# Loads of stored token sums moved within and between two DMA queues, and values staged through a wider ring of rows, in a hybrid convolution and attention step

## The chip, the cores and the metric

The kernel runs on one core of a Trainium2 chip. The metric is the device time of one execution, in microseconds (us). The times of before are three runs; one more execution was recorded by the hardware profiler, and all rows quoted below come from that one.

## The reference

One layer of a network is computed for two groups of tokens that share the weights: 128 prompt tokens and 512 latent tokens, 640 columns in all, with 1024 channels. Cut to what matters here:

```python
h = x * (1 + scale) + shift                      # modulation
z = h @ w_in                                     # 10 blocks of 1024 columns
hy, g_h, qkv, g_a, m = split(z)
hy = short_conv(hy)                              # 3 taps along the tokens
v_h, x1, x0 = split(hy); q, k, v = split(qkv)
y_h = (fft_conv(v_h * x1, filters) + v_h * x1 * d) * x0
y_a = attention(q, k, v)                         # window, context and prompt
p_h = (y_h * silu(g_h)) @ w_bh ; p_a = (y_a * silu(g_a)) @ w_ba
out = (sigmoid(m_h) * p_h + sigmoid(m_a) * p_a) @ w_out
y = layer_norm(alpha * x + gate * out)
```

The outputs are `y`, and the keys and values of the prompt.

## The kernel before, in words

All matrix products run on TensorE in a split form: each operand is kept as a high part and a low part, and a product is three matmuls (high by high, high by low, low by high). Tokens are the moving side in two halves of 320 columns, weights the stationary side in blocks of 128 by 128. `hH` and `hL` hold the high and low part of `h`, eight channel tiles of 128 by 640.

The work has three stages.

**Transform stage.** Projections for the convolution branch (`proj`, L183), the filter spectra and the transforms (`long_conv`, `long_conv_back`), and the values `v` (`values`, L656) are woven together; here a scheduler chooses the order of each engine's instructions. Beside it VectorE forms four sums of blocks of `h`: with `h` cut into 2 by 2 blocks (channel half by token half), `t1`, `t2`, `t3` and `t4` are sums and differences of those blocks. Each sum has four rows of 128 by 640 (320 KB): channel part 0 and 1 (the `r` in `load_sums(r, ...)`), each as a high and a low part. They are written to `tok_d` in device memory (`token_sums`, L725) and loaded back later. The name `t4_10` is the sum `t4`, part 1, high. The values of groups 1 to 3 go from PSUM through a staging tile (L688 to L690, ScalarE) to `v_d` in device memory (L691, L692).

**Attention stage.** From L1393 on the order of all engines and queues is the order in which the code is written (`manual_schedule`). A pair of weight tiles (256 output columns) is computed by `pair_tile` with seven products instead of eight, twelve matmuls each. Their moving operands, in this order, are those of `ORDER` (L1130): `("b11", "t2", "t3", "t1", "b21", "t4", "b22")`; a `b` is a block of `hH` and `hL` itself. So the second, third, fourth and sixth product of a pair read loaded sums. `operand` (L1122) gives the tile: in a product over a sum the four channel tiles `k` are taken in order, `k` 0 and 1 from the rows of part 0, `k` 2 and 3 from part 1, and for each `k` the matmuls read high, low, high. The four sums stay in SBUF for all 23 pairs; only the first pair meets them while they are being loaded. The weights of a pair are loaded plain by SyncE's queue (`ra`, `s2`, `rb`: `load_a`, `blocks`), and two blocks get a second weight block added to them by an accumulating DMA on GpSimd's queue (`summed`, L1163, L1164). `high` (ScalarE, L1185) and `low` (VectorE, L1193) make the split weights four products ahead; `sum1` (L1175) and `post` (L1210) are further VectorE work of a pair. `scratch` (L919) copies two half tiles of `hH` and of `hL` within SBUF.

**Last stage.** Branch projections, output projection and layer norm.

The loads that the change touches stand at three places: `hand_over` (L864) loads `t2` and `t3` of part 0; L1346 to L1348 load `t2` and `t3` of part 1 around the weights of the second pair (`load_b(1)`); L1398 to L1403 load `t1` and `t4` of both parts, behind `scratch()`. All of them go to SyncE's queue through `load_to` (L64). Each load takes a row from one of three pools: `yhp` (tag `yh`, nine rows, which also served x0, the products `yu` and the stored sums in the transform stage), `sp` (four rows `tr`) and `tp` (three rows `tr`); a load has to wait until the work that used this memory earlier is done. A DMA on SyncE's queue also waits for the one issued eight places before it to be complete, since eight semaphores are used in turn; GpSimd's queue has eight others.

Of the kernel before, what the change touches and what calls it, by code (L numbers as in the profile page):

```python
# [10 lines left out]
F32 = mybir.dt.float32  # L11
# [8 lines left out]
NK = 8  # L20
# [6 lines left out]
NG = LP + 1 + LS  # L27
# [19 lines left out]
def tile_hyena_natten_step(ctx: ExitStack, tc: tile.TileContext, a, o):  # L47
    nc = tc.nc
    P = 128

    def f(ap):
        return ap.bitcast(F32)
# [10 lines left out]
    def load_to(dst, src):  # L63
        ins = nc.sync.dma_start(dst, src)  # L64
        last[:] = [ins]
        if pinned[0]:
            tc.keep_in_program_order(ins)
# [38 lines left out]
    def row(pool, tag, name, dt=F32, bufs=NK + 1, n=NT):  # L106
        return pool.tile([P, NT + 4 if tag == "yh" else NT], dt, tag=tag, bufs=bufs, name=name)[:, :n]
# [548 lines left out]
    def values(m, home=None):  # L656
# [25 lines left out]
        if home is None:  # L682
            v = out[f"v{m}"] = slot(m, "v", f"v{m}")
            for c, p in ((0, parts[0]), (512, parts[1]), (1024, pe[:, :256])):
                nc.scalar.activation(v[:, c : c + p.shape[-1]], p, AF.Copy)
        else:
            for i, p in enumerate(parts):
                v = hwa.tile([P, NG + 1], F32, tag="cv", bufs=2, name=f"v{m}_{i}")  # L688
                nc.scalar.activation(v[:, :512], p, AF.Copy)  # L689
# [198 lines left out]
    ac = ctx.enter_context(ExitStack())  # L888
    edges, biases = {}, {}

    homes = []

    def load_sums(r, names):
        for name in names:
            for i in range(2):
                pool, tag, bufs = homes.pop(0) if r else (yhp, "yh", NK + 1)
                t = row(pool, tag, f"{name}_{r}{i}", F32R, bufs)
                tok[name][i].append(t)
                load_to(f(t), tok_d[4 * SUMS.index(name) + 2 * r + i])

    def attention_setup():
        nonlocal at, sp, tp
        hy.close()
        sp = ac.enter_context(tc.tile_pool(name="sp", bufs=1, reuse_waits="tile", side="right"))
        tp = left.enter_context(tc.tile_pool(name="tp", bufs=1, reuse_waits="tile"))
        homes[:] = [(sp, "tr", 4)] * 4 + [(tp, "tr", 3)] * 3 + [(yhp, "yh", NK + 1)]
# [487 lines left out]
    with tc.manual_schedule(engines=engines):  # L1394
        for _ in first_head():
            pass
        sums_of_second()
        scratch()  # L1398
        load_sums(0, SUMS[2:3])
        load_sums(1, SUMS[2:3])  # L1400
        load_a(1)
        load_sums(0, SUMS[3:])
        load_sums(1, SUMS[3:])  # L1403
        biases[0] = [bias_tile(h) for h in range(2)]
        for j in range(8):
            side, n_main, n_side = attend(j), N_PAIR * len(HEADS[j].split()), N_ATT if j < 7 else N_ATT + 3
# [323 lines left out]
```

## Time and profile before

| what | value |
|---|---|
| median of three runs | 885.01 us (885.0 to 885.81) |
| the profiled execution, its own time | 886.28 us |
| its span, first to last instruction | 884.5 us |
| mean granted TensorE clock | 0.992 |
| TensorE busy | 866.5 us, 98% |
| VectorE / ScalarE / GpSimd busy | 652.4 / 450.0 / 188.9 us |
| DMA queue of SyncE (q1): moved, share of the 16 DMA engines | 123.59 MB, 41.4% |
| DMA queue of GpSimd (q0): moved, share | 38.28 MB, 22.1% |

In rows of the timeline the columns are start, duration, engine, line, operation, output<-input, shape and count, and in brackets the idle time of the engine before it with what ended it. In rows of the table by windows they are the window, its length, then per engine the busy time with the number of instructions, the granted clock (PEclk), the mean busy share of the 16 DMA engines, and GB/s. In a list of waits they are the total in us, the number and the longest. Rows of DMA issues give the count, the size of one, and the median time in us from issue to landing. Tile numbers are left out, so that all sums read `t`.

### The profile page before, as it was taken

What the parts mean: (1) busy time and instruction counts of PE and PEld (TensorE: products, weight loads), DVE (VectorE), ACT (ScalarE), POOL (GpSimd) and SP (SyncE); (2) the same over time, 40 slices, a digit from 0 to 9 for tenths busy, and PEclk for the clock granted to TensorE, in tenths of its full rate; (3) what the DMA queues carried; (4) which work ended last, traced back from release to release, by engine and by line L of the source; (5) the groups of instructions that cost most, each with busy time, mean ns of one, the idle gap of its engine ahead of it and who ended that gap; (6) DMA issues with size and microseconds to landing.
All of it is one profiled execution on the core that took longest, in us unless ns stands there. A gap on an engine that the chain in (4) does not pass through costs nothing.

```text
span 884.5 us, 17176 instructions
## 1 busy us (share of the span) xinstructions
PE 866.5 (98%) x6452; PEld 836.1 (95%) x6452; DVE 652.4 (74%) x1243; ACT 450.0 (51%) x964; POOL 188.9 (21%) x216
## 2 busy tenths in 40 slices
PE   8999999999999997999999999999999999999996
PEld 6899999999999996999999999999999999999885
DVE  4778986596794855786877777777777487667666
ACT  4396465436555533666566656666666532243200
POOL 0012210110110111354353334333554200000000
PEclk9999999999999998999999999999999999999999
DMA  8978886456564778967676758675854587445521
GB/s 319 403 171 223 219 239 131 95 156 136 134 150 98 207 175 268 325 164 248 163 245 155 228 147 254 146 203 161 237 138 119 183 293 253 158 157 201 186 78 57
DMA packets 76110, 168.56 MB, mean 191 GB/s; under 512 B 11099, under 2 KB 29275, under 8 KB 76028
## 3 DMA queue, kind: packets, MB, share of 16 engines
q1 hardware_dynamic: 56780, 123.59, 41.4%
q0 software_dynamic: 13632, 38.28, 22.1%
q10 hardware_dynamic: 5616, 5.61, 1.9%
q8 instruction: 51, 0.84, 0.4%
q14 instruction: 31, 0.25, 0.1%
HBM read 142.80 MB, written 23.99 MB: 189 GB/s over the span
## 4 chain that ended last, share of the span: by engine, by line
PE 93%; DVE 3%; DMA 1%; ACT 1%; issue 0%; SPq 0%; POOL 0%; POOLq 0%; ACTq 0%
PE sp L1232 32%; PE mm L183 32%; PE out L1540 6%; PE v L669 4%; PE s L1044 2%; PE s L951 2%; PE pt L1035 2%; PE ve L680 1%; PE adaT L253 1%; DMA v_d<-v 1%; DMA t<-tok_d 1%; PE adaT L270 1%; PE yb L171 1%; PE yb L173 1%; PE yb L172 1%; PE ut L547 1%
## 5 line engine op out<-in xcount | busy, mean ns | idle before, releaser
L1232 PE MATMUL sp<-t,wb 128*128 128x320 f32 x1104 | 176.5, 313 | 5.4 <-DMA t<-tok_d 5.4
L1232 PEld LDWEIGHTS sp<-t,wb 128*128 128x128 f32 x1104 | 165.6, 189 | 7.3 <-issue 5.4
L1232 PE MATMUL sp<-hH,wb 128*128 128x320 f32 x548 | 132.9, 314 | 0.0
L1232 PEld LDWEIGHTS sp<-hH,wb 128*128 128x128 f32 x548 | 95.0, 190 | 2.6 <-issue 2.6
L1232 PE MATMUL sp<-hL,wb 128*128 128x320 f32 x274 | 85.1, 311 | 0.0
L163 POOL DMA_DIRECT2D wl<-wall x30 | 26.7, 890 | 239.2 <-ACT wl L162 174.8
L183 PE MATMUL mm<-hH,wh 128*128 128x320 f32 x288 | 69.4, 313 | 1.5 <-ACT v L689 0.8
L183 PE MATMUL mm<-hH,wl 128*128 128x320 f32 x288 | 69.5, 311 | 0.4 <-DVE wl L103 0.4
L183 PE MATMUL mm<-hL,wh 128*128 128x320 f32 x288 | 69.7, 311 | 0.0
L1193 DVE TENSOR_TENSOR wb<-s,wb 128x512 fp32r<-128x512 f32 x69 | 49.2, 714 | 22.7 <-ACT wb L1185 22.4
L1185 ACT ACTIVATE wb<-s 128x512 fp32r<-128x512 f32 x69 | 43.5, 632 | 35.7 <-PE sp L1232 20.2
L1006 POOL TENSOR_SCALAR edge<-edge,sm 128x320 f32<-128x320 f32 x32 | 42.1, 1437 | 68.0 <-DVE sm L1004 68.0
L1006 POOL TENSOR_SCALAR p<-p,sm 128x384 f32<-128x384 f32 x32 | 49.2, 1599 | 29.3 <-DVE sm L1004 14.5
L164 ACT ACTIVATE wh<-raw 128x1024 fp32r<-128x1024 f32 x30 | 31.9, 1063 | 42.0 <-PE mm L183 32.5
L1232 PEld LDWEIGHTS sp<-hL,wb 128*128 128x128 f32 x274 | 52.1, 190 | 0.0
L183 PEld LDWEIGHTS mm<-hH,wh 128*128 128x128 f32 x288 | 48.5, 188 | 3.0 <-ACT v L689 1.0
L183 PEld LDWEIGHTS mm<-hH,wl 128*128 128x128 f32 x288 | 48.9, 188 | 1.3 <-DVE wl L103 0.9
L183 PEld LDWEIGHTS mm<-hL,wh 128*128 128x128 f32 x288 | 49.0, 188 | 0.7 <-DVE hL L330 0.5
L1540 PE MATMUL out<-woh,yhs 128*128 128x512 f32 (+1 forms) x176 | 45.7, 373 | 0.0
L1220 DVE TENSOR_TENSOR spare_hHp<-sp,yu 128x320 f32<-128x320 f32 x69 | 33.4, 483 | 16.6 <-PE sp L1232 11.1
L183 PE MATMUL mm<-yhs,wh 128*128 128x320 f32 x224 | 42.6, 309 | 0.0
L1185 ACT ACTIVATE wb<-ra 128x512 fp32r<-128x512 f32 x46 | 29.1, 633 | 25.8 <-PE sp L1232 10.7
(412 smaller groups left out, 2251.1 us busy)
## 6 DMA issues: line engine op xcount, KB each, us to landing
raw<-wall SPq DMA_DIRECT2D x50, 512.0 KB, 3.8
wl<-wall POOLq DMA_DIRECT2D x30, 512.0 KB, 7.0
ra<-wall SPq DMA_DIRECT2D x23, 512.0 KB, 4.3
rb<-wall SPq DMA_DIRECT2D x44, 256.0 KB, 5.3
ada<-wada SPq DMA_DIRECT2D x16, 512.0 KB, 8.0
tm<-bias SPq DMA_DIRECT2D x16, 512.0 KB, 7.8
s<-wall SPq DMA_DIRECT2D x23, 256.0 KB, 4.9
s<-wall POOLq DMA_DIRECT2D x23, 256.0 KB, 4.4
```

What stands on the lines that cost most here:

```text
L163: nc.gpsimd.dma_start(wl, a["wall"][i], accum_op=ALU.add)
L164: nc.scalar.activation(wh, raw[:], AF.Copy)
L183: nc.tensor.matmul(ps[hf][:, :HALF], wt[k], x[:, hf * HALF : (hf + 1) * HALF], start=(i == 0 and k == 0), stop=(i == lead[2] and k == NK - ...
L669: nc.tensor.matmul(ps[t // 2][:, t % 2 * 256 : t % 2 * 256 + 256], x[:, k, P * t : P * t + P], wk, start=first and t % 2 == 0, stop=last, ...
L951: nc.tensor.matmul(dst[h], x[rows(h), qs], y[rows(h), ks], start=i == 0, stop=i == 2, skip_group_check=True)
L1006: nc.gpsimd.tensor_scalar_mul(pv, pv, sm[:, 2, c : c + 1])
L1035: nc.tensor.transpose(pt[:, i * P : i * P + P], ps[h][:, c : c + P], ident)
L1185: nc.scalar.activation(made[g][:, 0], block(g), AF.Copy)
L1193: nc.vector.tensor_tensor(made[g][:, 1], block(g), f(made[g][:, 0]), op=ALU.subtract)
L1220: nc.vector.tensor_tensor(c, dst, c if j == 3 else ps["u"], op=ALU.add)
L1232: nc.tensor.matmul(dst, wk, x(xi, k), start=j < 4 and k == 0 and i == 0, stop=k == 3 and i == 2, skip_group_check=True,)
L1540: ins = nc.tensor.matmul(dst, m[k][:, c0 : c0 + P], w[:, c : c + n], start=(first and k == 0), stop=(last and k == 5), skip_group_check=True,)
```

## The change

Three things are changed.

The loads of the sums are moved. `t2` and `t3` of part 1 are now loaded one after the other, and `t1` of both parts comes directly behind them, ahead of the plain weight loads of the second pair and ahead of `scratch`. `t4` of both parts is taken off SyncE's queue: GpSimd issues these four loads, behind its two accumulating loads for the second pair.

The homes are changed with it: `t1` takes the three rows of `tp` and one row of `yhp`, and `t4` takes four rows of `yhp`. Before, `tp` held `t1` of part 1 and one row of `t4`.

The values of groups 1 to 3 are staged in rows of the nine-row ring `yhp` instead of the two tiles `cv` of the pool `hwa`.

```diff
             for i, p in enumerate(parts):
-                v = hwa.tile([P, NG + 1], F32, tag="cv", bufs=2, name=f"v{m}_{i}")
+                v = row(yhp, "yh", f"v{m}_{i}", n=NG + 1)
...
-    def load_sums(r, names):
+    def load_sums(r, names, by=None):
...
-                pool, tag, bufs = homes.pop(0) if r else (yhp, "yh", NK + 1)
+                if r and name in SUMS[:2]:
+                    pool, tag, bufs = sp, "tr", 4
+                elif name == "t1" and (r, i) != (1, 1):
+                    pool, tag, bufs = tp, "tr", 3
+                else:
+                    pool, tag, bufs = yhp, "yh", NK + 1
...
+                if by is None:
+                    load_to(f(t), src)
+                else:
+                    by.dma_start(f(t), src)
...
-    load_sums(1, SUMS[:1])
+    load_sums(1, SUMS[:2])
+    for r in range(2):
+        load_sums(r, SUMS[2:3])
     sums_of_second = load_b(1)
-    load_sums(1, SUMS[1:2])
...
         sums_of_second()
+        for r in range(2):
+            load_sums(r, SUMS[3:], nc.gpsimd)
         scratch()
-        load_sums(0, SUMS[2:3])
-        load_sums(1, SUMS[2:3])
         load_a(1)
-        load_sums(0, SUMS[3:])
-        load_sums(1, SUMS[3:])
```

SyncE's queue before, at the passage from the transform to the attention stage, from the last two rows of `t3` on (`new_kT` is a store of keys, `hH` and `hL` are the copies of `scratch`, `ra1` is a weight tile of the second pair):

```order
L64 DMA t3_10_4037<-tok_d_81 128x640
L64 DMA t3_11_4039<-tok_d_81 128x640
L843 DMA new_kT<-kp0_4171 128x128
L64 DMA hH_85<-hHp_86 128x320 x2
L64 DMA hL_87<-hLp_88 128x320 x2
L64 DMA t1_00_4192<-tok_d_81 128x640
L64 DMA t1_01_4194<-tok_d_81 128x640
L64 DMA t1_10_4196<-tok_d_81 128x640
L64 DMA t1_11_4198<-tok_d_81 128x640
L64 DMA ra1_4200<-wall 128x1024
L64 DMA t4_00_4202<-tok_d_81 128x640
L64 DMA t4_01_4204<-tok_d_81 128x640
```

Two more rows of `t4` and the bias tiles `tm0` and `tm1` follow there. The same queue and place now (`s2_1` and `rb1` are the plain weight loads of the second pair, which before stood between `t2` and `t3`):

```order
L64 DMA t3_11_4034<-tok_d_81 128x640
L64 DMA t1_00_4036<-tok_d_81 128x640
L64 DMA t1_01_4038<-tok_d_81 128x640
L64 DMA t1_10_4040<-tok_d_81 128x640
L64 DMA t1_11_4042<-tok_d_81 128x640
L64 DMA s2_1_4045<-wall 128x512
L64 DMA rb1_4044<-wall 128x512 x2
L843 DMA new_kT<-kp0_4179 128x128
L64 DMA hH_85<-hHp_86 128x320 x2
L64 DMA hL_87<-hLp_88 128x320 x2
L64 DMA ra1_4208<-wall 128x1024
L64 DMA tm0_4210<-bias 128x1024
```

`t1` has moved ahead of the store of keys and of `scratch`, the weight loads have moved behind `t1`, and no row of `t4` is left on this queue. GpSimd's queue before, at the same passage (`yu` are products of the convolution branch, `edge` are cleared borders, L1163 and L1164 the accumulating loads of the second and then the third pair):

```order
L524 DMA yu_d_79<-yu6_3837 128x640
L524 DMA yu_d_79<-yu7_3842 128x640
L912 MEMSET edge00_3887 128x64
L912 MEMSET edge01_3889 128x64
L912 MEMSET edge30_3891 128x64
L912 MEMSET edge31_3893 128x64
L1163 DMA s2_1_4033<-wall 128x512
L1164 DMA rb1_4032<-wall 128x512
L1163 DMA s2_2_4292<-wall 128x512
L1164 DMA rb2_4291<-wall 128x512
```

And now, from the last cleared border on (line numbers are higher by six here):

```order
L918 MEMSET edge31_3893 128x64
L1169 DMA s2_1_4045<-wall 128x512
L1170 DMA rb1_4044<-wall 128x512
L906 DMA t4_00_4194<-tok_d_81 128x640
L906 DMA t4_01_4196<-tok_d_81 128x640
L906 DMA t4_10_4198<-tok_d_81 128x640
L906 DMA t4_11_4200<-tok_d_81 128x640
L1169 DMA s2_2_4292<-wall 128x512
L1170 DMA rb2_4291<-wall 128x512
```

The four rows of `t4` stand between the accumulating loads of the second and of the third pair. In the transform stage the scheduler sets many instructions of all engines in another order than before; from the first pair on the order of TensorE is the same as before, and that of VectorE and ScalarE but for a few rows at its start.

More of the change, by code (lines that the diff above doesn't have):

```diff
@@ L889, in tile_hyena_natten_step @@
     edges, biases = {}, {}
-    homes = []
-    def load_sums(r, names):
+    def load_sums(r, names, by=None):
         for name in names:
             for i in range(2):
-                pool, tag, bufs = homes.pop(0) if r else (yhp, "yh", NK + 1)
+                if r and name in SUMS[:2]:
[4 more added lines that the diff above has]
+                    pool, tag, bufs = yhp, "yh", NK + 1
                 t = row(pool, tag, f"{name}_{r}{i}", F32R, bufs)
                 tok[name][i].append(t)
-                load_to(f(t), tok_d[4 * SUMS.index(name) + 2 * r + i])
+                src = tok_d[4 * SUMS.index(name) + 2 * r + i]
+                if by is None:
+                    load_to(f(t), src)
+                else:
+                    by.dma_start(f(t), src)
     def attention_setup():
@@ L905, in attention_setup @@
         tp = left.enter_context(tc.tile_pool(name="tp", bufs=1, reuse_waits="tile"))
-        homes[:] = [(sp, "tr", 4)] * 4 + [(tp, "tr", 3)] * 3 + [(yhp, "yh", NK + 1)]
         at = ac.enter_context(tc.tile_pool(name="at", bufs=1, reuse_waits="tile", side="right"))
```

## The prediction

> **What bounds the kernel now.** The page comes first: which engine fills the span.
>
> ```profile
> PE 866.5 (98%) x6452; PEld 836.1 (95%) x6452; DVE 652.4 (74%) x1243; ACT 450.0 (51%) x964; POOL 188.9 (21%) x216
> ```
>
> TensorE is busy for 98% of 884.5 us, so only its idle time, and time at a lower clock, can be won. The list of TensorE's waits says for what it was idle.
>
> ```profile
> PE sp L1232 <- DMA t<-tok_d: 5.4, 4, 4.6
> ...
> PE mm L183 <- ACT v L689: 0.8, 1, 0.8
> PE fb L171 <- ACT sh L102: 0.5, 1, 0.5
> ```
>
> The first is what the change aims at, four waits for loaded sums; the second of the rows is a wait for a staging tile of the values, which the change touches too. TensorE's timeline shows the place of the four: the seven products of the first pair.
>
> ```profile
> 339.92 0.31 PE L1232 MATMUL sp<-hH,wb 128*128 128x320 f32 x1
> ...
> 341.68 3.71 PE L1232 MATMUL sp<-t,wb 128*128 128x320 f32 x24
> 350.03 0.61 PE L1232 MATMUL sp<-t,wb 128*128 128x320 f32 x1 [4.65 <-DMA t<-tok_d]
> ...
> 353.75 1.70 PE L1232 MATMUL sp<-t,wb 128*128 128x320 f32 x5 [0.18 <-DMA t<-tok_d]
> ...
> 358.19 1.92 PE L1232 MATMUL sp<-t,wb 128*128 128x320 f32 x12
> ...
> 361.80 0.33 PE L951 MATMUL s<-k,q 64*128 64x128 f32 x2
> ```
>
> The first product (no sum) takes 339.92 to 341.68, 12 matmuls, 0.147 us each. `t2` and `t3` follow without a gap and end at 345.39. Then `t1` is missing: four waits in one product, one per row. `t4` (358.19) waits for nothing, as the wait before it gave it time. The four products from 345.39 to the first attention matmul (361.80) take 16.4 us; at 0.147 us a matmul they would take 48 x 0.147 = 7.0. So 9.4 us is the most that this place can give. The windows of 2 us tell why it is more than the 5.4 of idle time, and what the DMA engines did meanwhile.
>
> ```profile
> 334.00:336.00 2.00, 2.00 (x15) 2.00 (x15) 1.30 (x3) 1.16 (x2) 0.00 (x0) 1.00 0.88 311
> ...
> 340.00:342.00 2.00, 2.00 (x16) 2.00 (x15) 1.65 (x8) 2.00 (x9) 1.89 (x7) 1.00 0.55 200
> ...
> 344.00:346.00 2.00, 1.39 (x10) 1.12 (x8) 2.00 (x5) 0.63 (x1) 0.00 (x0) 1.00 1.06 195
> ...
> 348.00:350.00 2.00, 0.00 (x0) 0.00 (x0) 0.05 (x1) 0.00 (x0) 0.00 (x0) 0.50 1.00 366
> ...
> 354.00:356.00 2.00, 2.00 (x8) 2.00 (x9) 0.26 (x1) 0.92 (x2) 0.00 (x0) 0.50 1.02 405
> 356.00:358.00 2.00, 2.00 (x9) 2.00 (x9) 1.90 (x5) 0.80 (x3) 0.00 (x0) 0.54 1.05 421
> ```
>
> After the gap the granted clock is 0.50 until about 357.85 (0.54 in the window to 358), some 4.1 us behind the last gap (353.75); a matmul then takes 0.268 us (8 or 9 in a 2 us window). And the DMA engines are as good as full from 344 on: shares of 1.00 to 1.06 in these rows. Only 340 to 342 has room, 0.55. So the place is limited by all that the 16 engines have to move, not by one queue's turn. This is what I weigh most.
>
> **The change, part by part.** First the fourth product's sums, `t1`. SyncE's timeline (start, duration of the issues) and the row for tile `t` give where they stood.
>
> ```profile
> 332.88 0.80 SPq L64 DMA_DIRECT2D t<-tok_d  x2
> ...
> 334.20 0.90 SPq L64 DMA_DIRECT2D rb<-wall  x2
> ...
> 341.16 1.17 SPq L64 DMA_DIRECT2D hH<-hHp  x2
> 342.37 1.93 SPq L64 DMA_DIRECT2D hL<-hLp  x2
> 344.43 4.05 SPq L64 DMA_DIRECT2D t<-tok_d  x4
> 348.52 0.43 SPq L64 DMA_DIRECT2D ra<-wall  x1
> 349.05 2.59 SPq L64 DMA_DIRECT2D t<-tok_d  x4
> 351.73 0.62 SPq L64 DMA_DIRECT2D tm<-bias  x1
> ```
>
> For all twelve rows of the three pools the trace has their first and last issue and the time to landing:
>
> ```profile
> L64 SPq DMA_DIRECT2D t<-tok_d x12: 325/468/1527, 332.9 to 351.0; - x12
> DMA to landing us min/median/max: 3.0/5.3/7.4
> ```
>
> `t1` was issued from 344.43 on, behind the copies of `scratch`. Now eight rows of 320 KB (2.62 MB) go out in a row from about 332 on; at the 0.311 MB/us of window 334 to 336 they need 8.4 us, the last lands at about 341. TensorE wants `t1` at 345.4. Even with 3 us lost to the stores of `yu` beside them they are in time: all four waits of `t1` go. The new order also puts seven more matmuls of the transform stage behind the last use of the memory that the loads take, so they can start 7 x 0.147 = 1.0 us earlier against the first product.
>
> What is late next is the sixth product, `t4`. TensorE comes to it at 345.4 + 24 x 0.147 = 348.9, after `t1` and a product without sums. Before, its last row was issued at 351.0 and, with the longest time to landing (7.4), was in at 358.4, close to where its product starts. Now GpSimd issues `t4` behind its accumulating loads, which need the plain loads of `s2` and `rb` that now stand behind `t1`.
>
> ```profile
> 340.01 1.23 POOL L524 DMA_DIRECT2D yu_d<-yu  x2 [19.15 <-DVE yu L475]
> 341.58 0.94 POOL L1163 DMA_DIRECT2D s<-wall  x1
> 342.15 1.28 POOL L1164 DMA_DIRECT2D rb<-wall  x1
> ...
> yu_d<-yu POOLq DMA_DIRECT2D x2, 320.0 KB, 3.4
> ...
> s<-wall POOLq DMA_DIRECT2D x1, 256.0 KB, 5.7
> rb<-wall POOLq DMA_DIRECT2D x1, 256.0 KB, 6.5
> ```
>
> Three plain loads of 256 KB (0.79 MB, 2.5 us at the same rate) land at about 343.5, so the accumulating loads go out at about 343.5 to 344.5 (before 341.58 and 342.15), and four issues of some 0.6 us put `t4` out from 344.5 to 347 or a little later (the homes of its last two rows also wait for the last stores of `yu`, issued at 340.01, 3.4 us to landing: 343.4 to 344.6, no later than that). The issue is 3 to 4 us earlier than before (349.05 to 351.0). But the landing is not: in front of the last row of `t4` the DMA engines still have to move the same bytes, the copies of `scratch`, the accumulating loads, `t1`, `ra`, `t4`. From 342 to 358.4 they were full, so I count their work: end before 358.4, less 0.9 for the idle part of 340 to 342 (2 us x 0.45), less 1.0 for the earlier start, plus what now overtakes. That is the two bias tiles `tm`, formerly behind `t4` on one queue, now beside it on the other. They are 512 KB each, 1.05 MB, 2.4 us at the 0.421 to 0.405 MB/us of 354 to 358. How much of them gets ahead depends on how the engines share two queues. The DMA table for 344.4 to 348.5, when both were loaded, reads:
>
> ```profile
> q0 software_dynamic: 278, 0.50, 69.6%
> q1 hardware_dynamic: 352, 0.48, 36.2%
> ```
>
> Equal bytes (0.50 and 0.48 MB) from both. GpSimd's queue holds 4 x 0.33 + 0.5 = 1.8 MB; SyncE's 0.64 (copies, 4 x 160 KB) + 0.52 (`ra`) = 1.2 MB before `tm`. By equal bytes about half of `tm` is moved when `t4` is in: +1.2, bounds 0 and 2.4. The last row of `t4` lands at 358.4 - 0.9 - 1.0 + 1.2 = 357.7 (356.5 to 358.9). The Trainium skill's page "DMA: Bandwidth & Descriptors", section "Issuing engines are not separate DMA queues", speaks against a gain from the other queue: loads started by different engines run on the same 16 engines and interleave, and only the issuing time is saved. The trace agrees, 69.6% and 36.2% filled the engines together; by that page alone the landing would be unchanged but for the order.
>
> TensorE then idles from 348.9 on for the rows of part 0, and runs at half clock behind the gap, as before for `t1`. Behind the last row stand half of a product and the seventh: 5 matmuls and 12, of which 15 fit into the 4.1 us at 0.268 and 2 go at 0.147: 4.4 us. End 357.7 + 4.4 = 362.1, against 361.80: **+0.3** (-0.9 to +1.5). The stall moves from the fourth product to the sixth and is not shortened.
>
> Second, the values.
>
> ```profile
> 199.53 0.60 ACT L689 ACTIVATE v<-v 128x512 f32<-128x512 f32 x1 [5.56 <-DMA v_d<-v]
> 200.18 0.41 PE L183 MATMUL mm<-hH,wh 128*128 128x320 f32 x1 [0.75 <-ACT v L689]
> ```
>
> ScalarE waited 5.56 us for the store of an earlier staging tile; TensorE behind it 0.75. With nine rows this goes: **-0.75**. In exchange rows of x0, `yu` and values wait for each other's stores; ScalarE is busy 51% and the other short wait of that list, on `sh`, is 0.5, so I take 0. The new order of the transform stage can gain little more than such a wait and lose two or three of them: 0, bounds -1.0 and +1.5 as an estimate.
>
> Sum: +0.3 - 0.75 = -0.45, and 886.28 becomes 885.8. The profiled execution lies 1.27 over the median; the prediction stands to the median: 885.01 - 0.45 = **884.6 us**, the likeliest case's own range 883.0 to 886.6 (landing bounds and a part of the re-ordering).
>
> **The rivals.** *A, `t4` comes early* (0.28). GpSimd's queue is served better than by equal bytes, or `tm` stays behind: the four rows land at most 6.5 us (the `rb` row) behind their issue at 347, so by 353.5. Then the second pair's `ra` is next: VectorE's `post` for the fifth product, which the seventh needs, stands behind the weights made from `ra`.
>
> ```profile
> ra<-wall SPq DMA_DIRECT2D x1, 512.0 KB, 6.5
> 355.08 0.63 ACT L1185 ACTIVATE wb<-ra 128x512 fp32r<-128x512 f32 x1 [10.31 <-DMA ra<-wall]
> ...
> 356.35 0.48 DVE L1220 TENSOR_TENSOR spare_hHp<-sp,spare_hHp 128x320 f32<-128x320 f32 x1
> ```
>
> With `ra` as late as before, the seventh product starts at 356.8 and ends at 358.6 to 360.0; with `ra` issued 4 us earlier, landing order decides and 357.9 (353.5 + 4.4) is the end. So -1.8 to -3.9; I take -2.0, as `ra` now shares the engines with `t4`. With the values: 885.01 - 2.75 = 882.3. For it speaks that before, `s` took only 5.7 and `rb` 6.5 us on that queue in the full stretch; against it, that 1.3 MB cannot go in 6 us through half of 0.4 MB/us.
>
> *B, `t4` comes later than before* (0.18). All of `tm` is moved ahead of the last row, and the earlier start is lost to the plain loads that hold up the accumulating ones: 358.4 + 2.4 = 360.8, end 365.2, +3.4, with the values +2.65: 887.7. It decides from a landing of 359.7 on. For it: `t4` is last on its queue and starts only when `s2` and `rb` are in. Against it: 0.9 us of idle engine time that the early loads must fill. The same skill page, section "Queues, rings and completion order", has each engine go round the queues packet by packet; no run here shows the turns by themselves, but by that rule the queue with larger packets gets more, and the table above has 1.8 KB a packet on GpSimd's queue and 1.4 on SyncE's, which is for A rather than B.
>
> *C, the transform stage loses* (0.09). A store of values, which took ScalarE 5.56 us of waiting, now holds a row that x0 or `yu` needs, and TensorE waits there: from 1.5 us on the kernel is slower. With a loss of 2.6, the +0.3 of the stall and no gain on the values it gives 887.9, near B's time. *The change does not do what it says* would be `t1`'s rows of `tp` becoming free too late; their earlier users stand far ahead of this place in the order, so 0.01, at 885.0.
>
> **How the numbers follow.** Forecast 0.44, A 0.28, B 0.18, C 0.09, no effect 0.01. A measurement of this kernel tells about 0.2%, 1.77 us. Faster by more than that, below 883.24: A, and 0.01 of the forecast's lower edge: 0.29. Slower, above 886.78: B and C: 0.27. Within: the rest of the forecast and no effect: 0.44. The range reaches from 881.6 (A with 357.9 and half of its sharing loss) to 888.0 (B and C, with 0.3 of re-ordering); outside remain A's best (-3.9 and -0.75: 880.4) and both losses together, 2 in 10.
>
> **What would show it.** Right: the first matmul of `t1` stands without brackets at about 345; brackets `<-DMA t<-tok_d` stand before the sixth product, from 348 on, the clock falls to 0.50 there, and attention starts within 1.2 us of 361.8 (less any shift of the first product); `t4` (now a row of GpSimd's queue) takes 8 to 12 us to landing; the wait on L689 is gone. Wrong: the sixth product starts before 353 (A), or `t4` lands behind 359.7 (B), or new waits of L183 appear between 90 and 340 (C). If `t1` still waits, the time of its loads was wrong.

## The result, and the profile after

The changed kernel takes 888.96 us (median, 888.34 to 890.08); before took 885.0 us beside it. The ratio is 1.0046, with a 95% interval of 1.0029 to 1.0064: slower, by 3.95 us. The forecast was 884.6 us and no change that can be measured, with a range up to 888.0. The profiled execution took 890.08 us (span 888.3), 3.8 more than the one of before, and all terms below are differences between these two.

TensorE's waits in the changed kernel, as a list of total, number and longest:

```profile
PE sp L1238 <- DMA t<-tok_d: 7.4, 3, 6.1
...
PE mm L183 <- ACT zs L486: 0.8, 1, 0.8
PE mm L183 <- ACT zs L485: 0.7, 1, 0.7
```

The wait for loaded sums has grown from 5.4 to 7.4 us, and the wait for a staging tile of the values (0.8) has gone, but two new ones of 0.8 and 0.7 stand in the list. TensorE's timeline of the first pair shows where the sums are waited for now:

```profile
340.72 0.31 PE L1238 MATMUL sp<-hH,wb 128*128 128x320 f32 x1
...
342.48 5.45 PE L1238 MATMUL sp<-t,wb 128*128 128x320 f32 x36
...
355.80 0.60 PE L1238 MATMUL sp<-t,wb 128*128 128x320 f32 x1 [6.11 <-DMA t<-tok_d]
357.29 2.17 PE L1238 MATMUL sp<-t,wb 128*128 128x320 f32 x6 [0.88 <-DMA t<-tok_d]
359.90 1.70 PE L1238 MATMUL sp<-t,wb 128*128 128x320 f32 x5 [0.44 <-DMA t<-tok_d]
...
364.73 0.47 PE L957 MATMUL s<-k,q 64*128 64x128 f32 x2
```

The row of 36 matmuls without a bracket is `t2`, `t3` and `t1`: the fourth product waits no more. The three rows with brackets are the sixth product. Attention starts at 364.73 instead of 361.80, 2.93 later. Of that, 0.80 was lost before the first product (340.72 against 339.92), and the stretch from the first product to attention takes 24.01 us instead of 21.88, 2.13 more. From there to the end of the execution, 890.08 - 364.73 = 525.35 against 886.28 - 361.80 = 524.48, another 0.87 is lost. 0.80 + 2.13 + 0.87 = 3.80.

The windows over the stall (window, length, busy time of the five engines, granted clock, DMA share, GB/s) answer to those of before:

```profile
352.00:354.00 2.00, 0.00 (x0) 0.00 (x0) 0.00 (x0) 0.14 (x1) 0.00 (x0) 0.50 1.04 345
...
360.00:362.00 2.00, 2.00 (x8) 2.00 (x9) 0.37 (x1) 0.32 (x1) 0.00 (x0) 0.50 0.77 285
362.00:364.00 2.00, 2.00 (x9) 2.00 (x8) 1.76 (x7) 1.36 (x6) 1.54 (x2) 0.50 0.03 9
364.00:366.00 2.00, 2.00 (x17) 1.67 (x18) 0.49 (x1) 1.09 (x2) 0.25 (x1) 0.65 1.02 165
```

The last column but one says most: the DMA engines are full up to 360 and then all but idle, 0.03 from 362 to 364. In the changed kernel the last row of `t4` lands near the end of this stretch (issued at 348.9, 11.0 us to landing: 359.9), and loads that nobody needs yet are moved ahead of it. SyncE's timeline names them:

```profile
345.78 0.83 SPq L64 DMA_DIRECT2D ra<-wall  x1
346.72 1.17 SPq L64 DMA_DIRECT2D tm<-bias  x2
...
348.68 0.76 SPq L64 DMA_DIRECT2D ra<-wall  x1
349.53 0.78 SPq L64 DMA_DIRECT2D s<-wall  x1
350.74 0.92 SPq L64 DMA_DIRECT2D rb<-wall  x2
```

GpSimd's timeline of the changed kernel shows when `t4` was issued:

```profile
344.21 0.89 POOL L1169 DMA_DIRECT2D s<-wall  x1 [1.52 <-DMA s<-wall]
346.36 0.88 POOL L1170 DMA_DIRECT2D rb<-wall  x1 [1.25 <-DMA rb<-wall]
346.92 2.51 POOL L906 DMA_DIRECT2D t<-tok_d  x4
```

Behind `ra` of the second pair (345.78) SyncE now issues not only the two bias tiles but, from 348.68 to 351.7, the weights of the third pair. In the kernel before, the same loads went out behind `t4`, by SyncE's timeline:

```profile
355.05 0.33 SPq L64 DMA_DIRECT2D ra<-wall  x1
355.86 0.33 SPq L64 DMA_DIRECT2D s<-wall  x1
356.65 1.15 SPq L64 DMA_DIRECT2D rb<-wall  x2
```

The DMA table of the changed kernel for the stretch in which `t4` is under way (347 to 360) has packets, MB and share of the engines:

```profile
q1 hardware_dynamic: 1118, 2.69, 57.2%
q0 software_dynamic: 557, 1.74, 45.8%
```

SyncE's queue (q1) moved 0.95 MB more than the queue that carried `t4`. The third pair's loads left 6.4 us earlier than before because a DMA on SyncE's queue waits for the one eight places ahead of it. Before, that one was, for the third pair's `ra`, the second pair's `ra`, which was in at 355.0 (issued at 348.52, 6.5 us to landing). With the four loads of `t4` gone it is the first copy of `scratch`; for the `s` behind it, it is the second, which was in at 349.4, and `s` left at 349.53.

### The profile page after: what moved, and what is told of

Read it like the earlier page. It is cut to its first block, busy times and chain, and to the rows that moved or that the text cites. A ratio compares the mean times of both kernels' runs of the same rounds, so it can differ in the third digit from the quotient of the medians.

```text
span 888.3 us, 17175 instructions
## 1 busy us (share of the span) xinstructions
PE 867.8 (98%) x6452; PEld 837.3 (94%) x6452; DVE 654.8 (74%) x1243; ACT 449.2 (51%) x964; POOL 190.9 (21%) x220
## 4 chain that ended last, share of the span: by engine, by line
PE 93%; DVE 3%; DMA 2%; ACT 1%; issue 0%; POOL 0%; POOLq 0%; ACTq 0%
PE sp L1238 32%; PE mm L183 31%; PE out L1545 6%; PE v L669 5%; PE s L1050 2%; PE s L957 2%; PE pt L1041 2%; PE ve L680 1%; DMA t<-tok_d 1%; PE adaT L253 1%; DMA yu_d<-yu 1%; PE adaT L270 1%; PE yb L171 1%; PE yb L173 1%; PE yb L172 1%; PE ut L547 1%
## 5 line engine op out<-in xcount | busy, mean ns | idle before, releaser
L183 PE MATMUL mm<-hH,wh 128*128 128x320 f32 x288 | 71.6, 314 | 2.3 <-ACT zs L486 0.8
L183 PE MATMUL mm<-hH,wl 128*128 128x320 f32 x288 | 70.6, 311 | 0.4 <-DVE wl L103 0.4
L183 PE MATMUL mm<-hL,wh 128*128 128x320 f32 x288 | 70.2, 311 | 0.0
L1012 POOL TENSOR_SCALAR p<-p,sm 128x384 f32<-128x384 f32 x32 | 48.3, 1554 | 29.6 <-DVE sm L1010 15.4
L183 PEld LDWEIGHTS mm<-hH,wh 128*128 128x128 f32 x288 | 49.1, 189 | 4.6 <-ACT zs L485 1.4
L183 PEld LDWEIGHTS mm<-hH,wl 128*128 128x128 f32 x288 | 49.1, 188 | 1.1 <-DVE wl L103 0.9
L183 PEld LDWEIGHTS mm<-hL,wh 128*128 128x128 f32 x288 | 49.0, 189 | 0.9 <-DVE hL L330 0.5
L183 PE MATMUL mm<-yhs,wh 128*128 128x320 f32 x224 | 42.7, 309 | 0.0
```

Of the source, the lines that this page charges most:

```text
L183: nc.tensor.matmul(ps[hf][:, :HALF], wt[k], x[:, hf * HALF : (hf + 1) * HALF], start=(i == 0 and k == 0), stop=(i == lead[2] and k == NK - ...
L1012: nc.gpsimd.tensor_scalar_mul(pv, pv, sm[:, 2, c : c + 1])
```

## The experiments

Two theories of the 2.13 us. **S (sharing)**: what SyncE's queue issues, no longer standing behind `t4`, takes the engines from it. **I (issue)**: `t4` is issued too late, behind accumulating loads that wait for `rb`. (The first expectation below also names a theory B, of the bytes ahead of `t4`; these runs do not tell it from S.) For the 0.80 us ahead of the first product: **V**, the values' new homes; **L**, the moved loads.

All runs together. The ratio is to before, measured anew beside each group of runs, with its 95% interval; runs of different groups are compared by it. The other columns are from the one profiled execution of each: when the first product starts, when the last group of matmuls of the sixth product starts after its last wait, and the time from the first product to attention. A start in brackets is one without a wait. Where eleven matmuls are left behind the last wait (355.75, 354.35 and 354.55 in the runs with `t1` early and with both held), that wait is for the second row of `t4` and the last row is in before TensorE asks for it; elsewhere it is for the last row. The profiled execution is often not the median one (its own time stands last), so that verdicts go by the ratio.

| run | median us | ratio | first product | last group of the sixth | to attention | profiled |
|---|---|---|---|---|---|---|
| before | 885.0 to 885.6 | 1 | 339.92 | (358.19) | 21.88 | 886.28 |
| changed | 888.96 | 1.0046 (1.0029 to 1.0064) | 340.72 | 359.90 | 24.01 | 890.08 |
| t1 early, t4 on SyncE behind ra | 885.20 | 0.9994 (0.9985 to 1.0003) | 340.22 | 354.35 | 19.15 | 884.14 |
| t4 on SyncE around ra | 885.91 | 1.0004 (0.9995 to 1.0013) | 341.91 | 358.43 | 21.07 | 887.74 |
| t4 ahead of the accumulating loads | 888.12 | 1.0033 (1.0020 to 1.0045) | 340.18 | 354.46 | 21.76 | 887.45 |
| bias and third pair held | 885.92 | 1.0006 (0.9997 to 1.0015) | 340.33 | 354.55 | 19.05 | 884.77 |
| third pair held | 888.52 | 1.0031 (1.0020 to 1.0041) | 341.14 | 359.75 | 22.11 | 888.52 |
| bias held | 887.62 | 1.0019 (1.0009 to 1.0028) | 341.26 | 357.60 | 21.14 | 887.58 |
| mirror | 892.33 | 1.0072 (1.0057 to 1.0087) | 340.35 | 362.34 | 26.57 | 892.10 |
| values alone | 886.27 | 1.0008 (0.9999 to 1.0017) | 341.90 | (358.92) | 20.64 | 886.95 |
| loads alone | 889.37 | 1.0038 (1.0026 to 1.0051) | 339.48 | 359.85 | 25.13 | 890.01 |
| t1 early, old values | 885.86 | 1.0002 (0.9993 to 1.0010) | 340.62 | 355.75 | 20.11 | 885.86 |
| split, held, old values | 889.25 | 1.0036 (1.0023 to 1.0050) | 339.13 | 355.93 | 21.51 | 886.41 |

**`t1` early, `t4` on SyncE's queue.** Against the changed kernel:

```diff
         sums_of_second()
-        for r in range(2):
-            load_sums(r, SUMS[3:], nc.gpsimd)
         scratch()
         load_a(1)
+        load_sums(0, SUMS[3:])
+        load_sums(1, SUMS[3:])
```

> The changed kernel, but t4 stays on SyncE's queue: behind scratch come ra of the second pair, the four rows of t4, then the bias tiles. Theory S (sharing): in the changed kernel t4 was late because SyncE's queue, freed of t4, ran ahead with the bias tiles and the third pair's weights and took 2.69 MB of the engines while GpSimd's queue moved 1.74 MB (347 to 360 us). Then here, with t4 ahead of them on one queue, its last row lands at about 356 instead of 359.8 and the kernel takes about 885.5 us, 3.5 less than the changed one. Theory I (late issue): t4 was late because it was issued at 346.9 to 349.4, behind accumulating loads that waited for rb. Here SyncE can issue it no earlier than about 346.5, so the time stays within 1 us of 888.96. Theory B (bytes): the engines' work up to t4's last row is what counts; it is less by tm and the third pair here too, so as S.

The time is 885.20 us and the gain over the changed kernel 0.0052 of 885, 4.6 us by the ratios. The last wait of the sixth product ends at 354.35. SyncE's timeline of this run:

```profile
345.82 2.30 SPq L64 DMA_DIRECT2D t<-tok_d  x4
348.22 1.32 SPq L64 DMA_DIRECT2D tm<-bias  x2
...
352.78 0.33 SPq L64 DMA_DIRECT2D ra<-wall  x1
```

And TensorE's, the sixth product and the first attention matmul:

```profile
353.61 0.39 PE L1238 MATMUL sp<-t,wb 128*128 128x320 f32 x1 [4.42 <-DMA t<-tok_d]
354.35 3.33 PE L1238 MATMUL sp<-t,wb 128*128 128x320 f32 x11 [0.36 <-DMA t<-tok_d]
...
359.37 0.33 PE L957 MATMUL s<-k,q 64*128 64x128 f32 x2
```

`t4` is issued from 345.82, 5.6 us after the first product, against 346.92 and 6.2 in the changed kernel. Its last row lands at 355.6 (issued at 347.7, 7.9 us), 15.4 us after the first product instead of 19.2. An issue 0.6 us earlier does not explain 3.8; the bias tiles are behind it now, and the third pair's weights go out at 352.78. So the whole loss of the changed kernel hangs on the queue of `t4`. That speaks for S, though `t4` also changed its queue and the way it is issued.

**Part 0 of `t4` ahead of `ra`, part 1 behind it**, on SyncE's queue:

```diff
         scratch()
+        load_sums(0, SUMS[3:])
         load_a(1)
-        load_sums(0, SUMS[3:])
-        load_sums(1, SUMS[3:])
+        load_sums(1, SUMS[3:])
```

(against the run before).

> As the run before, but part 0 of t4 stands ahead of ra of the second pair and part 1 behind it, on SyncE's queue. S: the sixth product starts at about 352 and waits a second time for part 1; ra then lands by 355 and the seventh product ends near 360; time about 884.5 us. I: issue of part 0 at about 345.5, 1.4 us earlier than in the changed kernel, so 1 to 1.5 less than it, about 887.5.

885.91 us: between the two expected times, 884.5 and 887.5, and not distinguishable from the run before. The sixth product does start a little earlier, 11.7 us after the first (353.59) instead of 13.4, but then it waits for part 1 until 358.43. In this profile, what is put ahead of `ra` is paid for by what comes behind it.

**`t4` ahead of the accumulating loads**, on GpSimd's queue; this takes away the late issue and leaves the sharing:

```diff
-        sums_of_second()
         for r in range(2):
             load_sums(r, SUMS[3:], nc.gpsimd)
+        sums_of_second()
```

> The changed kernel with one thing changed: GpSimd issues t4 ahead of its two accumulating loads of the second pair, not behind them. I: part 0 is then issued at about 342.5, 4.4 us earlier; part 1 once the yu stores are in, about 348; the sixth product starts 3 to 4 us earlier, the kernel takes about 886 us. S: SyncE's queue overtakes as before, and the accumulating loads now come behind t4, so that the second pair's sums hold up VectorE and with it the seventh product: no gain, 888 to 890 us.

888.12 us, about 1 us better than the changed kernel (0.0013 of 885), which is not clear of noise. The issue moved as I expected (342.06 and 346.18), and the sixth product started at 349.75 instead of 355.80. But the time did not follow. VectorE's timeline in this run says why:

```profile
349.15 0.49 DVE L1226 TENSOR_TENSOR spare_hHp<-sp,yu 128x320 f32<-128x320 f32 x1 [3.27 <-PE sp L1238]
356.63 0.69 DVE L1181 TENSOR_TENSOR s<-s,rb 128x512 f32<-128x512 f32 x1 [6.98 <-DMA s<-wall]
...
357.84 0.48 DVE L1226 TENSOR_TENSOR spare_hHp<-sp,spare_hHp 128x320 f32<-128x320 f32 x1
```

And TensorE's, the end of the sixth product and the start of the seventh:

```profile
354.46 1.70 PE L1238 MATMUL sp<-t,wb 128*128 128x320 f32 x5 [0.96 <-DMA t<-tok_d]
358.47 0.60 PE L1238 MATMUL sp<-hH,wb 128*128 128x320 f32 x1 [2.31 <-DVE spare_hHp L1226]
```

The accumulating loads now stand behind `t4`; `sum1` (L1181), which adds their results, is waited for until 356.63; behind it in VectorE's order stands `post`, which the seventh product needs. This is the chain of rival A, with the second pair's sums in the place of `ra`. The issue was late (I is right that far), but what waits for the accumulating loads is next, so that `t4` ahead of them won little here. What an earlier issue is worth by itself this run does not show, as it also delays the sums.

**What shares the engines with `t4`, held back.** In the changed kernel GpSimd issues the first two bias tiles, and the plain loads of the third pair, behind `t4` on its own queue:

```diff
-        load_to(tm[:], a["bias"][hd])
+        (nc.gpsimd.dma_start if hd < 2 else load_to)(tm[:], a["bias"][hd])
...
-    load_to(raws["a", p][:], a["wall"][pairs[p][0]])
+    (nc.gpsimd.dma_start if p == 2 else load_to)(raws["a", p][:], a["wall"][pairs[p][0]])
...
+        load = nc.gpsimd.dma_start if p == 2 else load_to
-        load_to(s2, w0[:, :512])
+        load(s2, w0[:, :512])
```

and so for the other two loads of `blocks`. Three runs: both changed, the third pair alone, the bias tiles alone.

> The changed kernel, but the first two bias tiles and the third pair's plain weight loads are issued by GpSimd, behind t4 on the same queue; SyncE's queue then has only scratch and ra beside t4. S: t4's last row lands near 355 instead of 359.8, TensorE's stall before the sixth product is 3 to 4 us shorter, time about 885 us. I: t4 is issued at 346.9 to 349.4 as before and the time stays at 888 to 889.5 us.

> The changed kernel, with the plain weight loads of the third pair (1.31 MB) issued by GpSimd behind t4; the first two bias tiles stay on SyncE's queue, beside t4. It splits the 3 us that the run with both held gained over the changed kernel. Theory S1: bytes count, whichever they are; the third pair's share of the 2.36 MB is 55%, so 1.7 us better than the changed kernel, about 887.3 us. Theory S2: the bias tiles come first on SyncE's queue and alone do the harm before t4's last row, since the third pair's loads are served behind them: no change, 888.5 to 889.

> The changed kernel, with the first two bias tiles (1.05 MB) issued by GpSimd behind t4, the third pair's loads still on SyncE's queue. S1: 45% of the gain, about 887.6 us. S2: nearly the whole gain of holding both, about 886.2 us, if the third pair's loads then are issued too late to take the engines from t4; but they move up in the queue into the place of the tiles, and then the gain is smaller than the tiles' share.

Held together: 885.92 us, ratio 1.0006; the loss is gone, although `t4` stays on GpSimd's queue, behind the same accumulating loads. So it is not that queue as such which is slow. The third pair alone: 1.0031, 1.3 us better than the changed kernel by the ratios, which is not clear of noise (1.0020 to 1.0041 against 1.0029 to 1.0064). The bias tiles alone: 1.0019, 2.4 better, just clear of it. Both at once: 3.5 (0.0040 of 885).

The times do not decide between S1 and S2. In the profiles the last row of `t4` takes 8.4 us from issue to landing with both held, 9.8 with only the tiles held, 10.8 with only the third pair held and 11.0 in the changed kernel (medians of the four rows: 8.6, 8.8, 10.6, 10.3). So the tiles alone beside `t4` cost 2.4 us, the third pair's loads alone 1.4, and both together only 2.6. The parts do not add, and the split by bytes of S1, 45% and 55%, is not what the profiles show. They lean to S2 with its own reservation: the tiles come first and do most of the harm, and without them the third pair's loads move up (they go out from 6.3 us after the first product instead of 8.0). These are single profiles.

In the profile of the run with both held, the last wait of the sixth product ends at 354.55. A row of TensorE's timeline there needs care in reading:

```profile
353.81 0.55 PE L1239 MATMUL sp<-t,wb 128*128 128x320 f32 x1 [4.51 <-DVE wb L1200]
354.55 3.13 PE L1239 MATMUL sp<-t,wb 128*128 128x320 f32 x11 [0.19 <-DMA t<-tok_d]
```

The bracket names VectorE's `wb`. But VectorE's timeline of the same run has the weights for this product and the next done long before:

```profile
344.35 0.68 DVE L1200 TENSOR_TENSOR wb<-rb_ql,wb 128x512 fp32r<-128x512 f32 x1
...
345.35 0.68 DVE L1200 TENSOR_TENSOR wb<-s,wb 128x512 fp32r<-128x512 f32 x1
```

The matmul reads `t4` and waits for several semaphores, of which one is named. The first row of `t4`, issued at 345.23, took 8.4 to 8.7 us to landing: 353.6 to 353.9, so that what the matmul stood still for was this load. Such brackets in the third-pair run (VectorE) and in the mirror (ScalarE) are to be read in the same way.

One reservation: in these three runs the second accumulating load went out 3.8 to 4.4 us after the first product, in the changed kernel 5.6. Nothing in their edits explains that. So 1.2 to 1.8 us of an earlier issue are mixed into their gain over the changed kernel, and theory I is not excluded as a smaller part. Compared with one another, two of them are free of it: `t4` goes out from 4.9 us after the first product with both held and from 5.0 with the third pair alone held (the last row at 7.4 and 7.8), and its last row lands 15.8 and 18.6 us after it. What their edits leave different is the place of the bias tiles. The next run tests the same from the other side.

**The mirror.** From the good order (`t1` early, `t4` on SyncE's queue behind `ra`), the same bias tiles and third-pair loads are given to GpSimd, where nothing of `t4` is ahead of them. The edit is the sum of the two above.

> The mirror image of the changed kernel: t1 early, t4 on SyncE's queue behind ra (as in the run of 885.20 us), and now the first two bias tiles and the third pair's plain loads are taken off that queue and issued by GpSimd, where nothing of t4 stands ahead of them. t4's issue is not touched. Theory S (two queues share the engines, so what no longer stands behind t4 in its own queue goes beside it): the slowdown of the changed kernel comes back, t4's last row lands 3 us later, time about 888 us. Theory I (the place and time of issue make t4 late): issue is as in the run of 885.20 us, so is the time. A third, P: SyncE's queue is simply served better than GpSimd's; then t4 loses little here, 885.5 to 886.5 us.

892.33 us, 0.0078 of 885 above the run without it: 6.9 us lost, where 3 were expected. By SyncE's timeline of this run `t4` is issued where it was:

```profile
346.20 2.80 SPq L64 DMA_DIRECT2D t<-tok_d  x4
```

GpSimd's has the loads that were taken off that queue:

```profile
344.82 1.64 POOL L950 DMA_DIRECT2D tm<-bias  x2
345.93 1.05 POOL L1144 DMA_DIRECT2D ra<-wall  x1
```

TensorE's has the last wait of the sixth product:

```profile
362.34 1.70 PE L1239 MATMUL sp<-t,wb 128*128 128x320 f32 x5 [1.16 <-DMA t<-tok_d]
```

The issue is 5.85 us after the first product (5.6 in the run without it), and the wait for the last row ends 22.0 us after it, where that row was in after 15.4. Theory I as the whole cause and theory P (SyncE's queue is served better) fall; S stands. The loss is larger than in the changed kernel, and a likely reason, not tested, stands in the rows: the tiles went out at 344.82, ahead of `t4` in time, and the third pair's loads from 345.93, where in the changed kernel they left from 348.68. The rows of DMA issues show it in one number, the median time from issue to landing of the four rows of `t4`. First the run with `t1` early and `t4` on SyncE's queue:

```profile
t<-tok_d SPq DMA_DIRECT2D x4, 320.0 KB, 7.6
```

With bias tiles and third pair held behind it on GpSimd's queue:

```profile
t<-tok_d POOLq DMA_DIRECT2D x4, 320.0 KB, 8.6
```

In the changed kernel:

```profile
t<-tok_d POOLq DMA_DIRECT2D x4, 320.0 KB, 10.3
```

And in the mirror:

```profile
t<-tok_d SPq DMA_DIRECT2D x4, 320.0 KB, 11.8
```

Short where both groups of loads stand behind `t4` in one queue, long where both run beside it, on either queue.

**The values, and the loads, alone.** The first is the kernel before with the one line of the values changed; the second is the changed kernel with that line as before.

```diff
-                v = hwa.tile([P, NG + 1], F32, tag="cv", bufs=2, name=f"v{m}_{i}")
+                v = row(yhp, "yh", f"v{m}_{i}", n=NG + 1)
```

> The kernel before with the values staged in the nine-row ring; no load is moved. Theory V: the new homes of the values reorder the transform stage, and two waits of 0.8 and 0.7 us on ScalarE's zs copies take the place of the one on the values; the first product starts at about 340.7 instead of 339.9 and the time is about 885.8 us. Theory L: those 0.8 us come from the moved loads; then this kernel gains the wait of 0.75 us, about 884.3 us.

> The changed kernel with the values staged in the two tiles of before; only the loads are moved. V: the first product starts at 339.9, the sixth product's stall is as long as in the changed kernel, time about 888.1 us. L: the first product starts at 340.7 or later, and the wait for the value's tile is there as well, about 889.7 us.

The values alone: 886.27 us, 1.0008 (0.9999 to 1.0017); the loads alone: 889.37 us, 1.0038 (1.0026 to 1.0051); the whole change 1.0046. The loads carry the loss; what the values add, 0.7 us, is not clear of zero. The waits show what happened to the forecast gain. TensorE's waits with the values alone:

```profile
PE mm L183 <- DMA wl<-wall: 1.2, 1, 1.2
PE mm L183 <- ACT zs L486: 0.8, 1, 0.8
PE mm L183 <- ACT zs L485: 0.7, 1, 0.7
```

The two waits on `zs` come with the values' new homes (they are in all nine profiled kernels that have them and in none of the four that don't), and the wait they replace was one of 0.3 to 1.0. V is right on that. The 1.2 on `wl`, a weight load, is in some profiles and not in others.

But the new order has a second effect, which works against it. With the values in the ring, the loads of sums start 8.1 us ahead of the first product (332.65 against 340.72 in the changed kernel; 333.83 against 341.90 with the values alone); without, 7.0 us (332.44 against 339.48 with the loads alone; 332.88 against 339.92 before). That is the 1.0 us of head start of the prediction, and the stretch up to attention is shorter by 1.2 where only the values differ (20.64 against 21.88) and by 1.1 (24.01 against 25.13). About 0.8 lost ahead of the first product and 1.1 won behind it: this fits that the time hardly moves.

**The best of both?** `t1` early, `t4` on SyncE's queue behind `ra`, values in their old tiles (the two edits above):

> t1 early, t4 on SyncE's queue behind ra as in the earlier run, and the values staged in the two tiles of before. If the values' new homes cost 0.9 us, as the run with them alone showed, and the early t1 with t4 on SyncE gains the rest, this is the best: the first product at about 339.5 instead of 340.2, time 884.2 us, ratio 0.999. If the two do not add, 885.2 us.

885.86 us, 1.0002 (0.9993 to 1.0010). Expected was 884.2 if the parts add, and they do not. Part of it is the reason just given (to attention 20.11 instead of 19.15); and the first product starts at 340.62, not at the 339.5 that was expected, with a wait of 1.0 us for a staging tile of the values in TensorE's list. So the 0.8 us ahead of the first product is not the same in every profile. No version of these beats the kernel before by more than a measurement can tell; the lowest ratio is the 0.9994 of the first run.

**Part 0 of `t4` first, then the accumulating loads, then part 1, the rest held**, all on GpSimd's queue, with the old values:

> GpSimd's queue takes, in this order: part 0 of t4, the two accumulating loads of the second pair, part 1 of t4, the first two bias tiles and the third pair's plain loads; values in the two tiles of before. If the late landing of t4 and the chain over the second pair's sums (VectorE, seventh product) are all there is, both are served here: the sixth product starts 2 us earlier than where t4 stood behind the accumulating loads with both held, and the time is 883.5 us. If the engines' bytes bind (all of it must land by the seventh product), it ends like the run with both held, less the 0.9 for the values: 885 us.

889.25 us, 1.0036, against 883.5 or 885: both expectations failed. The profiled execution is the fastest of its eight (886.41; the slowest took 890.87), so it shows only part of it. In it the sixth product starts at 350.06 but waits again until 355.93 for part 1, which was issued at 346.52 to 347.8, and VectorE waited 4.6 us for the copies of `hH`, longer than the 3.15 in the changed kernel. The likely reading, argued and not shown: early bytes for part 0 were late bytes for the copies, the sums and part 1. Why the other executions are 1 to 4 us slower still, no profile shows.

## Why the prediction was wrong, step by step

**`t1` waits no more**: right, 36 matmuls without a gap. **The stall moves to the sixth product, with half clock behind it**: right; it starts at 355.80 after 6.11 us of idle time, and the clock is 0.50 from 352 to 364. **The head start of 1.0 us**: right (7.0 to 8.1 us). **8 to 12 us to landing for `t4`**: right, 8.7 to 11.0. Of the 4.25 us that the profiled execution lies above its forecast (890.08 against 885.83), 1.83 is the stall, 1.55 the values and 0.87 lies behind attention.

**`t4` issued from 344.5 to 347**: 2 us too early. It went out from 346.92, since the last plain load of `rb` held up the accumulating load until 346.36; I had put its landing at 343.5. 0.8 of that is the later first product. That this lateness was not the main cause is shown by the runs in which `t4` is issued alike and lands 2.8 us apart (both held, and the third pair alone held).

**The landing at 357.7** is the step that failed, by its term of +1.2 us (0 to 2.4) for what overtakes `t4`. The last row landed at 359.9, or 359.1 with the first product where it was, 1.4 above the forecast and 0.2 above its bound. The sum let half of the bias tiles overtake. The second tile was in at 359.1 (issued at 347.4, 11.7 us to landing), ahead of `t4`'s last row, so both overtook in full. And the sum put the third pair's weights, 1.31 MB, at nothing: it asked what stands behind `t4` on SyncE's queue in the list shown, and not what SyncE does when `t4` is no longer there. They had been issued behind `t4`, from 355.05, and now left from 348.68; 0.59 MB of them were moved after 360, so some 0.7 MB before.

The run with both groups held has the landing without this overtaking: 356.1 (issued at 347.7, 8.4 us), or 355.7 with its first product where it was. Without the +1.2 the sum has 356.5. So what is ahead of `t4` was priced 0.8 too high, and the overtaking cost 2.6 (by the time to landing, 11.0 against 8.4) to 3.4 (by the place of the landing) instead of 1.2; that the landing was missed by only 1.4 is in part luck. The tiles alone are 2.4 to 2.8 of it; the weights beside them add 0.2 to 0.6.

"By equal bytes" was wrong as well: SyncE's queue moved 2.69 MB and GpSimd's 1.74 from 347 to 360. The stretch from which it was read had 0.50 and 0.48 MB, but 278 and 352 packets. The rule that queues are gone round packet by packet (the Trainium skill, "DMA: Bandwidth & Descriptors", section "Queues, rings and completion order") agrees with the trace where both queues had work waiting: from 354 to 358 they moved 258 and 268 packets, and GpSimd's, with the larger ones, more bytes (1.06 and 0.59 MB). The sign drawn from it, that this speaks for an early `t4`, did not come true, as over the whole stretch GpSimd's queue moved less: 93 packets against 369 from 347 to 350, and 24 against 271 from 358 to 360, when `t4` was all but in.

**4.4 us from the last row to attention** became 4.83: the granted clock was still 0.50 up to 364 and 0.65 in the window from 364 to 366, so that it came back at about 365.4, 5.5 us behind the last gap instead of 4.1. All 17 matmuls ran at 0.268, not 15, and the first five took 0.16 more than that. 0.3, the 1.4 of the landing and these 0.43 make the 2.13.

**-0.75 for the values** became +0.80: the wait went, and two others came, on `zs`, a loss that the prediction had bounded (+1.5) but taken as 0. Measured alone, the values are +0.7 us and not clear of zero, and the loads +3.4 where +0.3 was forecast; so the landing weighs most. **Nothing behind attention** became +0.87; about 0.3 is half clock that reaches into the first attention scores (the first product of the second pair starts 3.25 us later than before, attention 2.93). The rest is spread over 520 us and not explained; the other runs have between -0.1 and 1.3 there.

**The rivals.** A's condition (an early `t4`) was brought about by hand, and its chain then did hold the seventh product, though through the sums. B, at 0.18, came nearest: a late landing and a slower kernel, for one of that rival's two reasons, all of the tiles ahead of the last row. But with the first product where it was the landing was 359.1, short of its 359.7, and attention started at 363.9 instead of 365.2; that its 887.7 lies near the measured time is in part luck, as C's kind of loss came with it: two new waits on L183, though 0.80 us and not the 1.5 from which C counts. The range, 881.6 to 888.0, ended 1 us too low. The statement of the Trainium skill that the forecast cites for the other view ("DMA: Bandwidth & Descriptors", section "Issuing engines are not separate DMA queues"), that loads from different engines interleave on the same 16 engines and another issuer saves issuing time only, agrees with the runs: with both groups behind `t4`, SyncE's queue gives 885.20 us and GpSimd's 885.92. The runs add the part that hurts: a queue is also an order, and a load taken out of it loses its place ahead of what followed.

## What to carry to other kernels

When a load is moved to another queue, write down two lists: what it now stands behind, and what on the old queue stood behind it and will now run beside it, on through the next stage's prefetches, until that queue waits for something. Where the DMA engines are full, as here, a late load was helped by holding back what is needed later, not by the other queue. And an earlier order of some loads has to be followed to every consumer in the stretch: here part 0, `ra`, the sums and the copies took turns at being last.

## What the runs showed of the hardware that I had not expected

From 354 to 358 two queues that both had work waiting shared the engines packet by packet and not byte by byte. In the changed kernel GpSimd's queue and SyncE's moved 258 and 268 packets, with 1.06 and 0.59 MB. In the same four microseconds of four other runs the packets are 262 and 256 (third pair held), 237 and 237 (bias tiles held), 284 and 282 (mirror), 271 and 277 (loads alone), with 1.06 and 0.57, 0.94 and 0.67, 0.99 and 0.64, 1.11 and 0.56 MB. So in these stretches a load beside another queue's loads gets about every second packet, and the queue with the larger packets gets more of the bytes. This fits that the two groups beside `t4` do not add up: as long as the other queue has packets waiting, it takes its turns. Earlier in the stretch it was otherwise: from 347 to 350 the changed kernel has 93 packets with 0.17 MB against 369 with 0.67. The DMA table for the first stretch:

```profile
q1 hardware_dynamic: 369, 0.67, 73.6%
q0 software_dynamic: 93, 0.17, 30.4%
```

And for the second:

```profile
q0 software_dynamic: 258, 1.06, 66.0%
q1 hardware_dynamic: 268, 0.59, 37.8%
```

In the first stretch GpSimd's queue still had the last accumulating load ahead of `t4` (issued at 346.36, in at 354.1). Why it moved so few packets then, no run separates.
